# Mixer: the first head projected and activated ahead of the second half of the gates' chain, its queries, scores and an output gate ahead of the rows' transposes

## The chip, the cores and the metric

The kernel runs on one core of a Trainium2 chip. The metric is device time in microseconds (us); a kernel's time is the median of its runs. The core has five engines that run at the same time, each with its own queue: TensorE (PE, with its weight loads shown as PEld), VectorE (DVE), ScalarE (ACT), GpSimd (POOL) and SyncE (SP), which here issues most DMAs.

## The reference, cut to what matters

One layer of a diffusion backbone: a half-step SwiGLU, a mixer, another half-step SwiGLU, each between two RMS norms with modulation. There are 512 latent tokens and 256 context tokens of width 1024. The change lies in the mixer:

```python
p = y @ w_in                      # y: 768 tokens x 1024; columns: u (512), v (512), o (512), gates (16), pooling (512)
u = silu(short_conv(p_u))         # 3 taps along the tokens, 4 heads of 128
q, k = u @ w_q, u @ w_k           # per head
ig, fg = p_gates + biases         # 2 directions x 4 heads
# per direction and head, in chunks of 128 tokens:
#   b = cumsum(log_sigmoid(fg));  a running maximum m_t of decayed ig;  decays exp(.. - m_t)
#   num, den from (q k^T masked and decayed) v  and from a carried state;  h = num / max(|den|, exp(-m_t))
mix = concat(norm(h) * sigmoid(p_o), pool(p_pool))    # pool: box means of windows 2, 4, 8, 16 on the 8 x 64 grid
x = x + gate * norm(mix @ w_out)
```

## The kernel before, in words

**Products.** All large products are float32 split in a high and a low part, so each is three matmuls (`mm3p`). The normalised, modulated tokens lie as `yh`, `yl` (width across the partitions, 768 tokens along). A projection of 128 columns reads 8 weight blocks: `wcols` loads 1024 x 128 weights into a `raw` buffer (5 of them, by SP) and splits them (`split_w`) by a cast on ACT (L81) and a subtraction on DVE (L78) into two of 8 `wins` buffers, so that four sets of weights are there at a time.

**Stages.** The first SwiGLU ends, `values` projects v and the 16 gate columns (banks `pa`, `pz`, `pt` of PSUM: 4, 2 and 2). Then comes the mixer:

1. *The gates' chain* (L929 to L987), 64 rows x 768 tokens: three transposes twice, a log-sigmoid (ACT Exp L938 and Ln L939), two prefix sums on DVE (L950, L952), small copies that put the chunks' totals in place (L955 to L958), then what the change calls `gates`: three running-maximum scans (L959, L961, L963), small adds and copies into `mc` (L969 to L975), an Exp of `mc` (L976), the subtraction L978 and Exp L979 that make the rows `tr`, L980 to L983 for the rows' second half and for `br`, and `negmu` (L985 to L987). The order is by data: each step needs the one ahead of it.
2. *Rows to columns* (`rows_to_columns`): six transposes of `tr` in two `pt` banks, DVE copies out of them (L1011), four transposes of `br` in a third `pt` tile, copies (L1017), a selection matrix `sel` (L1022), `bd` (L1023), one small matmul and `cs_b` (L1028). All weights of keys, decays and states need these columns.
3. *Projections*: `u` is a head's input u (256 then 512 tokens, copied to `up` by ACT L1121, after DVE has zeroed its edges at L1117; then the convolution: ACT L1124 and two DVE instructions L1127; then ACT Silu L1129), `g` an output gate, `p` a pooling group. A group's sums run on POOL (L1053, L1100, L1101). `z` is the first half of the output product.
4. *Heads*: for each of the 4 heads queries `q` (a matmul, its ACT copy `qT` L1165, six transposes, two ACT copies L1171), scores `k` (four matmuls on `qT`, DVE products with the masks L1181), and for both directions weights `w`, states `s`, decays `d`, outputs `o`; then norm `n` and back `t`.

**Order.** `QUEUE` lists the projections, as generators that give PE one weight block of work at a time; `MIX` lists the heads' steps by letter, head and direction. `f2.4` draws some 2.4 us of work from the queue, `f` without a number draws until a pause (`.`), `R` is rows to columns, `P` a pooling group's second half. Matmuls and transposes of these steps keep the order of the program. On the other engines a planner sets the order ahead of time: among the instructions that its own model of the times takes as ready, the one that stands earlier in the program goes first. The order of each queue is then fixed, and an instruction that waits holds up those behind it. `tc.issue_after(x)` places what its block traces on `x`'s engine behind `x` in that engine's queue; it is an order, not a wait. Tiles of the mixer (`h` in the trace) come from `h4`, 16 buffers.

So before, PE gets pooling group 3, `u0` and `u1` ahead of `R`, then head 0's queries; the whole gates' chain stands ahead of all of these in the program.

Of the kernel before, what the change touches and what calls it, by code (L numbers as in the profile page):

```python
# [8 lines left out]
F32 = mybir.dt.float32  # L9
F32R = mybir.dt.float32r  # L10
# [6 lines left out]
P = 128  # L17
# [22 lines left out]
MIX = "f R q0 w00 f2.4 k0 s00 w01 d00 f0.4 f1.1 d01 s01 f3.35 o00 f3.45 q1 P3 o01 w10 k1 w11 f5.7 f2.25 s10 f0.1 f0.4 d10 s11 n0 f3.9 d11 f5.05 o10 f2.05 q2 w21 t0 P2 f2.8 w20 o11 n1 k2 f0.1 f0.1 s20 f2.95 d20 t1 f2.35 s21 d21 f2.15 o20 f1.6 P1 f1.25 o21 n2 f1.3 q3 w30 f2.15 t2 f1 w31 k3 d30 s30 f1.35 d31 s31 f2.65 o30 f0.1 f1.55 o31 n3 f0.1 f2 f0.1 P0 t3 f"  # L40


@with_exitstack
def tile_layer(ctx: ExitStack, tc: tile.TileContext, x, c, ctxt, c_ctx, w_mod, b_mod, norm_pre, norm_post,
# [855 lines left out]
    with ExitStack() as sx:  # L900
# [41 lines left out]
        def ch(tl, p0=0, p1=R):  # L942
# [15 lines left out]
        V.tensor_copy(ch(dr, 32, R)[:, 5:6, P - 1:P], ch(br, 32, R)[:, 0:1, 0:1])  # L958
        V.tensor_tensor_scan(out=mu[lo, 0:NT], data0=dr[lo, 0:NT], data1=ir[lo, 0:NT], initial=0.0,  # L959
                             op0=ALU.add, op1=ALU.max)  # L960
        V.tensor_tensor_scan(out=mu[hi, 0:NCTX][:, ::-1], data0=dr[hi, 0:NCTX][:, ::-1], data1=ir[hi, 0:NCTX][:, ::-1],  # L961
                             initial=0.0, op0=ALU.add, op1=ALU.max)
        V.tensor_tensor_scan(out=mu[hi, NCTX:NT][:, ::-1], data0=dr[hi, NCTX:NT][:, ::-1],  # L963
                             data1=ir[hi, NCTX:NT][:, ::-1], initial=mu[hi, 0:1], op0=ALU.add, op1=ALU.max)
# [4 lines left out]
        V.tensor_add(mcv[lo, 1:6], ch(dr, 0, 32)[:, 1:6, 0:1], ch(mu, 0, 32)[:, 0:5, P - 1:P])  # L969
        V.tensor_add(mcv[hi, 0:1], ch(dr, 32, R)[:, 0:1, P - 1:P], ch(mu, 32, R)[:, 1:2, 0:1])  # L970
        V.tensor_add(mcv[hi, 2:5], ch(dr, 32, R)[:, 2:5, P - 1:P], ch(mu, 32, R)[:, 3:6, 0:1])
        V.tensor_add(mcv[hi, 5:6], ch(dr, 32, R)[:, 5:6, P - 1:P], ch(mu, 32, R)[:, 0:1, 0:1])
        V.tensor_copy(mcv[lo, 12:18], ch(mu, 0, 32)[:, :, P - 1:P])
        V.tensor_copy(mcv[hi, 12:18], ch(mu, 32, R)[:, :, 0:1])
        V.tensor_sub(mc[:, 6:12], mc[:, 0:6], mc[:, 12:18])  # L975
        S.activation(out=mc[:, 6:12], in_=mc[:, 6:12], func=AF.Exp)  # L976

        V.tensor_sub(ch(tr), ch(ir), mcv[:, 12:18].broadcast_to([R, 6, P]))  # L978
        S.activation(out=t_, in_=t_, func=AF.Exp)  # L979
        V.tensor_copy(tr[R:2 * R, 0:NT], i_)  # L980
        LA = slice(NCTX, NT)
        V.tensor_add(br[0:R, LA], br[0:R, LA], mu[0:R, LA])
        S.activation(out=br[0:R, LA], in_=br[0:R, LA], func=AF.Exp, scale=-1.0)  # L983
        negmu = pool.tile([2 * R, NLAT], F32R, name="negmu")
        V.tensor_scalar_mul(mu[0:R, LA], mu[0:R, LA], -1.0)  # L985
        S.copy(negmu[0:R], mu[0:R, LA])
        V.tensor_sub(negmu[R:2 * R], mu[0:R, LA], negmu[0:R].bitcast(F32))  # L987

# [12 lines left out]
        bd = pool.tile([R, 8, 12], F32, name="bd")  # L1001
        cs_b = pool.tile([P, 8, 12], F32, name="cs_b")
        def rows_to_columns():

            for half in range(2):
                p = pt()
                for j in range(3):
                    tp(out=p[:, j * P:(j + 1) * P], in_=tr[:, (3 * half + j) * P:(3 * half + j + 1) * P],
                                identity=ident)
                for a in range(2):  # L1010
                    V.tensor_copy(tcol[:, 3 * half:3 * half + 3, a],  # L1011
                                  p[:, 0:384].rearrange("p (c a d r) -> p c a d r", c=3, a=2, d=2)[:, :, a, :, 0:4])
# [6 lines left out]
            selm = ident[0:R, 0:R].rearrange("p (d r) -> p d r", d=2)[:, :, 0:4]  # L1019
            for d in range(2):  # L1020
                for half in range(2):
                    V.tensor_copy(sel[half * R:(half + 1) * R, 4 * d:4 * d + 4], selm[:, d])  # L1022
# [27 lines left out]
        idhs, ups, uas, ogs = {}, {}, {}, {}  # L1050

# [3 lines left out]
        def pool_front(g):  # L1055

            win = WINDOWS[g]
            wts = wcols(PCOL + g * P)
            A = h4()[:, 0:GROWS * PW].rearrange("p (r c) -> p r c", c=PW)
# [406 lines left out]
```

## Time and profile before

| | |
|---|---|
| median of 3 runs | 1161.06 us (1160.05 to 1162.71) |
| the profiled execution | 1160.3 us |
| its span, first to last instruction | 1158.6 us |
| mean granted TensorE clock | 0.988 |
| busy: PE, PEld | 1107.9 us (96%), 1002.4 us (87%) |
| busy: DVE, ACT, POOL | 886.3 us (76%), 522.9 us (45%), 104.6 us (9%) |
| chain that ended last | PE 76%, DVE 9%, DMA 6%, ACT 3%, issue 2%, POOL 1% |

Busy is the time in which an engine ran at least one instruction. The granted clock is TensorE's as the throttle gave it, as a share of full speed. The chain is followed back from the last instruction, at each step to what released it. A row of a timeline gives a start, a duration, the engine, the source line, the operation and its operands, and in brackets how long the engine had been idle and what ended that.

### The profile page before, as it was taken

Reading aid. Unit: us, or ns where it says so; the run is one execution under the profiler, and the core shown is the slowest. Engines: PE = TensorE matmul, PEld = TensorE weight load, DVE = VectorE, ACT = ScalarE, POOL = GpSimd, SP = SyncE. Lnnn points to the kernel's source line nnn. Section 1 sums busy time; section 2 is a strip of 40 time slices with the busy share of each in tenths; the row PEclk is TensorE's granted clock in tenths of the full one; section 3 lists DMA queues with packets and bytes.
Section 4 is the critical chain, followed back from the end, with each engine's and each line's share of the span. In section 5 each row is a group of like instructions: output and inputs, shape, how many; then the busy total and the mean of one; then the engine's idle time right before and its main releaser. Section 6 shows DMA issues by size and latency. Waiting matters only on the chain.

```text
span 1158.6 us, 17190 instructions
## 1 busy us (share of the span) xinstructions
PE 1107.9 (96%) x6610; PEld 1002.4 (87%) x6610; DVE 886.3 (76%) x1309; ACT 522.9 (45%) x904; POOL 104.6 (9%) x139
## 2 busy tenths in 40 slices
PE   4999999999999999999899799999999999999996
PEld 2799999999998787888798687878899998999995
DVE  4698998898995685537628868856899998888865
ACT  4534333334333442326544755548554443444431
POOL 4000000000000000200205054211000000000001
PEclk9999999999999999999999899999999999999998
DMA  9943443542735896338513112135245544333321
GB/s 308 264 138 95 149 132 117 190 131 93 221 125 158 313 355 214 108 138 292 161 34 100 41 61 89 57 129 164 75 126 146 152 136 137 110 109 110 109 74 73
DMA packets 151807, 166.09 MB, mean 143 GB/s; under 512 B 7318, under 2 KB 125590, under 8 KB 151724
## 3 DMA queue, kind: packets, MB, share of 16 engines
q1 hardware_dynamic: 144708, 154.18, 42.0%
q10 hardware_dynamic: 7016, 10.80, 2.7%
q8 instruction: 52, 0.85, 0.3%
q14 instruction: 31, 0.25, 0.1%
HBM read 149.98 MB, written 14.98 MB: 142 GB/s over the span
## 4 chain that ended last, share of the span: by engine, by line
PE 76%; DVE 9%; DMA 6%; ACT 3%; issue 2%; POOL 1%; ACTq 0%; SPq 0%; DVEq 0%; POOLq 0%
PE pa L98 16%; PE pa L99 16%; PE pa L97 15%; PE pa L102 10%; PE pz L102 5%; PE pz L97 4%; DMA m<-in_w_mod_dram 3%; PE pz L98 3%; PE pz L99 3%; PE pt L102 3%; DVE wins L78 1%; DVE m L694 1%; PE pt L105 1%; ACT junk L148 1%; DMA raw<-in_w_mod_dram 1%
## 5 line engine op out<-in xcount | busy, mean ns | idle before, releaser
L97 PE MATMUL pa<-yh,wins 128*128 128x256 f32 (+1 forms) x768 | 236.4, 308 | 0.9 <-ACT pu L375 0.5
L98 PE MATMUL pa<-yh,wins 128*128 128x256 f32 (+1 forms) x768 | 235.9, 307 | 0.1
L99 PE MATMUL pa<-yl,wins 128*128 128x256 f32 (+1 forms) x768 | 235.6, 307 | 0.0
L78 DVE TENSOR_TENSOR wins<-raw,wins 128x1024 fp32r<-128x1024 f32 (+1 forms) x132 | 141.6, 1074 | 60.2 <-ACT wins L81 31.1
L81 ACT CAST wins<-raw 128x1024 fp32r<-128x1024 f32 (+1 forms) x134 | 123.0, 925 | 100.4 <-PE pa L99 35.0
L97 PEld LDWEIGHTS pa<-yh,wins 128*128 128x128 f32 x768 | 144.6, 188 | 4.1 <-ACT pu L375 1.1
L98 PEld LDWEIGHTS pa<-yh,wins 128*128 128x128 f32 x768 | 144.8, 188 | 0.9 <-DVE wins L78 0.3
L99 PEld LDWEIGHTS pa<-yl,wins 128*128 128x128 f32 x768 | 144.8, 189 | 0.3
L98 PE MATMUL pa<-th,wins 128*128 128x384 f32 (+1 forms) x388 | 121.9, 315 | 0.5 <-DVE wins L78 0.5
L99 PE MATMUL pa<-tl,wins 128*128 128x384 f32 (+1 forms) x388 | 122.2, 315 | 0.0
L97 PE MATMUL pa<-th,wins 128*128 128x384 f32 (+1 forms) x388 | 121.7, 315 | 0.0
L694 DVE SCALAR_TENSOR_TENSOR m<-m,sc,m 128x1024 f32<-128x1024 f32 x72 | 90.1, 1279 | 25.4 <-DMA m<-in_w_mod_dram 22.0
L81 ACT CAST wins<-sw 128x1024 fp32r<-128x1024 f32 x78 | 81.7, 1049 | 59.1 <-PE pa L99 33.9
L78 DVE TENSOR_TENSOR wins<-sw,wins 128x1024 fp32r<-128x1024 f32 x78 | 95.1, 1221 | 10.6 <-PE pa L98 8.6
L102 PE MATMUL pa<-yh,wins 128*128 128x512 f32 (+2 forms) x352 | 97.1, 362 | 0.0
L97 PEld LDWEIGHTS pa<-th,wins 128*128 128x128 f32 x388 | 72.9, 188 | 1.2 <-issue 0.8
L98 PEld LDWEIGHTS pa<-th,wins 128*128 128x128 f32 x388 | 73.2, 189 | 0.7 <-DVE wins L78 0.7
L99 PEld LDWEIGHTS pa<-tl,wins 128*128 128x128 f32 x388 | 73.1, 188 | 0.1
L102 PEld LDWEIGHTS pa<-yh,wins 128*128 128x128 f32 x352 | 62.1, 191 | 9.2 <-issue 2.2
L102 PE MATMUL pa<-yl,wins 128*128 128x512 f32 (+2 forms) x176 | 62.3, 354 | 0.0
L97 PE MATMUL pz<-wos,gh 128*128 128x512 f32 x144 | 56.6, 393 | 1.6 <-DVE z L429 1.1
L98 PE MATMUL pz<-wos,gl 128*128 128x512 f32 x144 | 56.3, 391 | 0.0
(409 smaller groups left out, 2198.0 us busy)
## 6 DMA issues: line engine op xcount, KB each, us to landing
raw<-in_ffn_w_in_dram SPq DMA_DIRECT2D x87, 512.0 KB
raw<-in_ffn_w_out_dram SPq DMA_DIRECT2D x56, 512.0 KB
m<-in_w_mod_dram SPq DMA_DIRECT2D x49, 512.0 KB
raw<-in_w_mod_dram SPq DMA_DIRECT2D x19, 512.0 KB
g<-q SPq DMA_DIRECT2D x22, 384.0 KB
q<-g ACTq DMA_DIRECT2D x44, 192.0 KB
raw<-in_w_in_dram SPq DMA_DIRECT2D x16, 512.0 KB
raw<-in_w_out_dram SPq DMA_DIRECT2D x16, 256.0 KB
```

The lines of the kernel that those rows point to most:

```text
L78: return eng.tensor_tensor(out=out_ap, in0=a, in1=b, op=ALU.subtract)
L81: return S.copy(hi, src)
L97: T.matmul(out_ap, lhsT=wh, rhs=xh, start=first, stop=False, **kw)
L98: T.matmul(out_ap, lhsT=wl, rhs=xh, start=False, stop=False, **kw)
L99: T.matmul(out_ap, lhsT=wh, rhs=xl, start=False, stop=last, **kw)
L102: return tc.keep_in_program_order(T.matmul(*args, **kw))
L105: return tc.keep_in_program_order(T.transpose(**kw))
L148: return S.activation(out=junk, in_=src, func=AF.Square, scale=D ** -0.5, accum_out=ssq)
L694: V.scalar_tensor_tensor(out=accs[st], in0=w, scalar=sc[:, st * KD + k:st * KD + k + 1], in1=accs[st], op0=ALU.mult, op1=ALU.add)
```

## The change

The second half of the gates' chain (from the first running-maximum scan on) becomes a function, `gates`, that is called at a new step `A`. The queue's first item is now `u0`, then a pause; `MIX` begins `f A f q0 k0 R w00`: draw `u0`, step `A`, draw group 3, `u1` and the output gate `g0`, then head 0's queries and scores, then rows to columns. Step `A` first makes the weights of group 3, of `u1` and of `g0` (`prefetch`), then traces `gates` behind head 0's Silu and behind the high cast of `g0`'s weights; both are on ACT, so both order ACT alone. In rows to columns the third and the fourth PSUM tile come from `pa` and `pz` instead of `pt`; the `sel` copies are traced ahead of it. `h4` gets 17 buffers. Seven numbers of `MIX` change: the first draw behind `w00` goes from 2.4 to 4.4, and six later ones become smaller by 0.6 to 1.8 each, 6.4 together.

```diff
-HB = 16
+HB = 17
-QUEUE = "p3 u0 u1 . u2 g0 p2 u3 g1 p1 g2 g3 p0 z"
-MIX = "f R q0 w00 f2.4 k0 s00 w01 d00 f0.4 f1.1 d01 s01 f3.35 o00 f3.45 q1 P3 o01 w10 k1 w11 f5.7 f2.25 s10 f0.1 f0.4 d10 s11 n0 f3.9 d11 f5.05 o10 f2.05 q2 w21 t0 P2 f2.8 w20 o11 n1 k2 f0.1 f0.1 s20 f2.95 d20 t1 ...
+QUEUE = "u0 . p3 u1 g0 . u2 p2 u3 g1 p1 g2 g3 p0 z"
+MIX = "f A f q0 k0 R w00 f4.4 s00 w01 d00 f0.4 f1.1 d01 s01 f3.35 o00 f2.45 q1 P3 o01 w10 k1 w11 f3.9 f2.25 s10 f0.1 f0.4 d10 s11 n0 f2.9 d11 f3.75 o10 f2.05 q2 w21 t0 P2 f2.1 w20 o11 n1 k2 f0.1 f0.1 s20 f2.35 d20 t1 ...
...
-        V.tensor_tensor_scan(out=mu[lo, 0:NT], ...
+        def gates():
+            V.tensor_tensor_scan(out=mu[lo, 0:NT], ...
...
+            V.tensor_sub(negmu[R:2 * R], mu[0:R, LA], negmu[0:R].bitcast(F32))
...
+        selm = ident[0:R, 0:R].rearrange("p (d r) -> p d r", d=2)[:, :, 0:4]
+        for d in range(2):
+            for half in range(2):
+                V.tensor_copy(sel[half * R:(half + 1) * R, 4 * d:4 * d + 4], selm[:, d])
         def rows_to_columns():
...
-            p = pt()
+            p = pa()
             for j in range(4):
                 tp(out=p[:, j * R:(j + 1) * R], in_=br[0:R, NCTX + j * P:NCTX + (j + 1) * P],
...
-            p = pt()
+            p = pz()
             mm(p[:, 0:96], lhsT=ones[0:R].broadcast_to([R, P]), rhs=bd..., start=True, stop=True)
...
+        casts = []
         def wcols(c0):
-            wh, wl = split_w(load_cols(w_in, c0))
+            wh, wl = split_w(load_cols(w_in, c0), keep=casts.append)
+        early_w = {}
+        def weights_of(c0):
+            return early_w.pop(c0, None) or wcols(c0)
+        def prefetch():
+            for c0 in (PCOL + 3 * P, P, 2 * M_W):
+                early_w[c0] = wcols(c0)
...
-            S.activation(out=u0, in_=u0, func=AF.Silu)
-            uas[h] = ua
+            silu = S.activation(out=u0, in_=u0, func=AF.Silu)
+            uas[h], silus[h] = ua, silu
...
+            elif what == "A":
+                prefetch()
+                with tc.issue_after(silus[0].ins), tc.issue_after(casts[-2].ins):
+                    gates()
```

`head_u`, `pool_front` and `out_gate` call `weights_of` in place of `wcols`.

## Rows read from the trace of the kernel before

**Rows 1.** The page's first part: busy time, share and instructions of each engine
```profile
PE 1107.9 (96%) x6610; PEld 1002.4 (87%) x6610; DVE 886.3 (76%) x1309; ACT 522.9 (45%) x904; POOL 104.6 (9%) x139
```

**Rows 2.** Windows: stretch, its length, busy of five engines, granted clock, DMA share, GB/s
```profile
638.00:640.00 2.00, 0.72 (x6) 0.64 (x6) 1.98 (x9) 1.62 (x3) 0.00 (x0) 0.99 0.00 0
640.00:650.00 10.00, 5.73 (x22) 4.22 (x21) 6.96 (x16) 8.30 (x13) 0.00 (x0) 0.50 0.30 71
650.00:760.00 110.00, 108.22 (x613) 91.29 (x613) 84.21 (x199) 63.85 (x147) 36.97 (x35) 1.00 0.20 64
```

**Rows 3.** Timeline of PE, 613 to 670: start, duration, engine, line, operation [idle before]
```profile
613.07 0.71 PE L102 MATMUL pa<-yh,wins 128*128 128x512 f32 x2
...
618.73 0.40 PE L102 MATMUL pa<-yh,wins 128*128 128x256 f32 x2
...
627.14 0.40 PE L102 MATMUL pa<-yh,wins 128*128 128x256 f32 x2
...
639.28 0.95 PE L105 MATMUL pt<-ident,h 128*128 128x128 f32 x6 [3.64 <-ACT h L979]
644.50 0.66 PE L105 MATMUL pt<-ident,h 64*128 64x64 f32 x4 [4.27 <-DVE tcol L1011]
...
645.57 2.07 PE L102 MATMUL pz<-h,wqk 128*128 128x512 f32 x2
...
648.58 0.78 PE L102 MATMUL pa<-yh,wins 128*128 128x256 f32 x2
...
652.22 1.05 PE L102 MATMUL pz<-h,h 128*128 128x128 f32 x8
653.11 1.28 PE L102 MATMUL pt<-vx,h 128*128 128x129 f32 x10
...
668.06 1.02 PE L102 MATMUL pz<-h,wqk 128*128 128x512 f32 x2
...
669.57 1.02 PE L102 MATMUL pz<-h,wp 128*128 128x512 f32 x2
```

**Rows 4.** Timeline of DVE, 619 to 696
```profile
619.08 0.95 DVE L940 SCALAR_TENSOR_TENSOR h<-h,h 64x768 f32<-64x768 f32 x1 [1.43 <-ACT h L939]
...
621.15 2.78 DVE L950 TENSOR_TENSOR_SCAN h<-h,h 32x768 f32<-32x768 f32 x1
...
629.66 2.31 DVE L959 TENSOR_TENSOR_SCAN h<-h,h 32x768 f32<-32x768 f32 x1
632.01 0.77 DVE L961 TENSOR_TENSOR_SCAN h<-h,h 32x256 f32<-32x256 f32 x1
...
635.26 1.16 DVE L970 TENSOR_TENSOR mc<-h,h 32x1 f32<-32x1 f32 x1
...
642.09 2.08 DVE L1127 SCALAR_TENSOR_TENSOR h<-h,pcol,h 128x770 f32<-128x770 f32 x2 [0.53 <-ACT h L1124]
...
694.34 1.78 DVE L1127 SCALAR_TENSOR_TENSOR h<-h,pcol,h 128x770 f32<-128x770 f32 x1
```

**Rows 5.** Timeline of POOL, 620 to 637
```profile
620.54 6.98 POOL L1053 TENSOR_TENSOR h<-h 128x624 f32<-128x624 f32 x3 [25.66 <-ACT h L1066]
...
634.34 2.07 POOL L1101 TENSOR_TENSOR h<-h,h 128x512 f32<-128x512 f32 x1
```

**Rows 6.** Timeline of ACT, 628 to 649
```profile
628.18 1.28 ACT L976 ACT_TABLE_LOAD   x1
...
638.38 0.84 ACT L979 ACTIVATE h<-h 64x768 f32<-64x768 f32 x1 [0.72 <-DVE h L978]
...
640.16 0.84 ACT L1121 COPY h<-pa 128x256 f32<-128x256 f32 x2
641.03 1.03 ACT L1124 ACTIVATE h<-h,pcol 128x770 f32<-128x770 f32 x1
...
647.68 0.59 ACT L1165 COPY h<-pz 128x512 f32<-128x512 f32 x1 [0.28 <-PE pz L102]
```

**Rows 7.** Timeline of SP's queue: issues of the projections' weights
```profile
559.11 19.86 SPq L114 DMA_DIRECT2D raw<-in_w_in_dram  x5
```

More of the change, by code (lines that the diff above doesn't have):

```diff
@@ L38 @@
 STEPS = "X0 E0 X1 X2 H00 Q0 H01 N0 N1 r00 G01 X3 r01 X4 N2 r02 r03 N3 b0 X5 Q1 N4 c0 N5 s01 y01 r10 E1 r11 s00 r12 r13 y00 b1 H10 G00 A10 H11 c1 Q2 A00 L11 G10 s11 y11 r20 A20 r21 r22 r23 A11 s10 y10 Q3 b2 c2 s20 y20 A21 r30 r31 r32 r33 A01 b3 s21 c3 s30 A02 y30 A22 y21 s31 A23 A03 y31 A12 A13"
-QUEUE = "p3 u0 u1 . u2 g0 p2 u3 g1 p1 g2 g3 p0 z"
-MIX = "f R q0 w00 f2.4 k0 s00 w01 d00 f0.4 f1.1 d01 s01 f3.35 o00 f3.45 q1 P3 o01 w10 k1 w11 f5.7 f2.25 s10 f0.1 f0.4 d10 s11 n0 f3.9 d11 f5.05 o10 f2.05 q2 w21 t0 P2 f2.8 w20 o11 n1 k2 f0.1 f0.1 s20 f2.95 d20 t1 f2.35 s21 d21 f2.15 o20 f1.6 P1 f1.25 o21 n2 f1.3 q3 w30 f2.15 t2 f1 w31 k3 d30 s30 f1.35 d31 s31 f2.65 o30 f0.1 f1.55 o31 n3 f0.1 f2 f0.1 P0 t3 f"
+QUEUE = "u0 . p3 u1 g0 . u2 p2 u3 g1 p1 g2 g3 p0 z"
+MIX = "f A f q0 k0 R w00 f4.4 s00 w01 d00 f0.4 f1.1 d01 s01 f3.35 o00 f2.45 q1 P3 o01 w10 k1 w11 f3.9 f2.25 s10 f0.1 f0.4 d10 s11 n0 f2.9 d11 f3.75 o10 f2.05 q2 w21 t0 P2 f2.1 w20 o11 n1 k2 f0.1 f0.1 s20 f2.35 d20 t1 f2.35 s21 d21 f2.15 o20 f1.6 P1 f1.25 o21 n2 f1.3 q3 w30 f2.15 t2 f1 w31 k3 d30 s30 f1.35 d31 s31 f2.65 o30 f0.1 f1.55 o31 n3 f0.1 f2 f0.1 P0 t3 f"
 @with_exitstack
@@ L958, in tile_layer @@
         V.tensor_copy(ch(dr, 32, R)[:, 5:6, P - 1:P], ch(br, 32, R)[:, 0:1, 0:1])
[L959 to L964, printed above, removed]
         mc = const.tile([R, 18], F32, name="mc")
@@ L968, in tile_layer @@
         mcv = mc.rearrange("p (a b) -> p a b", b=1)
[L969 to L980, printed above, removed]
-        LA = slice(NCTX, NT)
-        V.tensor_add(br[0:R, LA], br[0:R, LA], mu[0:R, LA])
-        S.activation(out=br[0:R, LA], in_=br[0:R, LA], func=AF.Exp, scale=-1.0)
@@ L984, in tile_layer @@
[L984 to L987, printed above, removed]
+        negmu = pool.tile([2 * R, NLAT], F32R, name="negmu")
+        LA = slice(NCTX, NT)
+        def gates():
+            V.tensor_tensor_scan(out=mu[lo, 0:NT], data0=dr[lo, 0:NT], data1=ir[lo, 0:NT], initial=0.0,
+                                 op0=ALU.add, op1=ALU.max)
+            V.tensor_tensor_scan(out=mu[hi, 0:NCTX][:, ::-1], data0=dr[hi, 0:NCTX][:, ::-1], data1=ir[hi, 0:NCTX][:, ::-1],
+                                 initial=0.0, op0=ALU.add, op1=ALU.max)
+            V.tensor_tensor_scan(out=mu[hi, NCTX:NT][:, ::-1], data0=dr[hi, NCTX:NT][:, ::-1],
+                                 data1=ir[hi, NCTX:NT][:, ::-1], initial=mu[hi, 0:1], op0=ALU.add, op1=ALU.max)
+            V.tensor_add(mcv[lo, 1:6], ch(dr, 0, 32)[:, 1:6, 0:1], ch(mu, 0, 32)[:, 0:5, P - 1:P])
+            V.tensor_add(mcv[hi, 0:1], ch(dr, 32, R)[:, 0:1, P - 1:P], ch(mu, 32, R)[:, 1:2, 0:1])
+            V.tensor_add(mcv[hi, 2:5], ch(dr, 32, R)[:, 2:5, P - 1:P], ch(mu, 32, R)[:, 3:6, 0:1])
+            V.tensor_add(mcv[hi, 5:6], ch(dr, 32, R)[:, 5:6, P - 1:P], ch(mu, 32, R)[:, 0:1, 0:1])
+            V.tensor_copy(mcv[lo, 12:18], ch(mu, 0, 32)[:, :, P - 1:P])
+            V.tensor_copy(mcv[hi, 12:18], ch(mu, 32, R)[:, :, 0:1])
+            V.tensor_sub(mc[:, 6:12], mc[:, 0:6], mc[:, 12:18])
+            S.activation(out=mc[:, 6:12], in_=mc[:, 6:12], func=AF.Exp)
+            V.tensor_sub(ch(tr), ch(ir), mcv[:, 12:18].broadcast_to([R, 6, P]))
+            S.activation(out=t_, in_=t_, func=AF.Exp)
+            V.tensor_copy(tr[R:2 * R, 0:NT], i_)
+            V.tensor_add(br[0:R, LA], br[0:R, LA], mu[0:R, LA])
+            S.activation(out=br[0:R, LA], in_=br[0:R, LA], func=AF.Exp, scale=-1.0)
+            V.tensor_scalar_mul(mu[0:R, LA], mu[0:R, LA], -1.0)
+            S.copy(negmu[0:R], mu[0:R, LA])
+            V.tensor_sub(negmu[R:2 * R], mu[0:R, LA], negmu[0:R].bitcast(F32))
@@ L1017, in rows_to_columns @@
             V.tensor_copy(gcol, p[:, 0:4 * R].rearrange("p (c d r) -> p c d r", c=4, d=2)[:, :, :, 0:4])
-            selm = ident[0:R, 0:R].rearrange("p (d r) -> p d r", d=2)[:, :, 0:4]
             for d in range(2):
-                for half in range(2):
-                    V.tensor_copy(sel[half * R:(half + 1) * R, 4 * d:4 * d + 4], selm[:, d])
                 V.tensor_tensor(out=bd[:, 4 * d:4 * d + 4],
@@ L1043, in project @@
                 yield n * 1.275e-3
+        casts = []
         def wcols(c0):
-            wh, wl = split_w(load_cols(w_in, c0))
+            wh, wl = split_w(load_cols(w_in, c0), keep=casts.append)
             return kc(wh), kc(wl)
+        early_w = {}
[4 more added lines that the diff above has]
+                early_w[c0] = wcols(c0)
         PW = GW + 16
-        idhs, ups, uas, ogs = {}, {}, {}, {}
+        idhs, uas, ogs, silus = {}, {}, {}, {}
         def padd(o, a, b):
@@ L1057, in pool_front @@
             win = WINDOWS[g]
-            wts = wcols(PCOL + g * P)
+            wts = weights_of(PCOL + g * P)
             A = h4()[:, 0:GROWS * PW].rearrange("p (r c) -> p r c", c=PW)
@@ L1112, in head_u @@
         def head_u(h):
-            wts = wcols(h * P)
+            wts = weights_of(h * P)
             up = h4()
@@ L1128, in head_u @@
                                        in1=u0, op0=ALU.mult, op1=ALU.add)
-            S.activation(out=u0, in_=u0, func=AF.Silu)
-            uas[h] = ua
+            silu = S.activation(out=u0, in_=u0, func=AF.Silu)
+            uas[h], silus[h] = ua, silu
         def out_gate(h):
-            wts = wcols(2 * M_W + h * P)
+            wts = weights_of(2 * M_W + h * P)
             q = pa()
```

## The prediction

> **What bounds the kernel now.** I read the page first: PE is busy 96% of the span [rows 1], so time is to be had only where PE idles or runs slowly. Cutting the mixer into windows finds one such place: in 640 to 650 PE is busy for 5.73 us of 10, and its granted clock is 0.50, the lower of two levels (1.2 of 2.4 GHz); in the 110 us behind it PE is busy for 108.22 at clock 1.00 [rows 2]. PE's timeline then shows three losses one behind the other [rows 3]:
>
> - Group 3, `u0` and `u1` are through at about 635.6. The transposes of the rows start at 639.28, after 3.64 us in which PE waits for ACT's Exp L979, the end of the gates' chain.
> - The next transposes start at 644.50, after 4.27 us. Both `pt` banks are taken, and the copies that empty them (L1011) stand on DVE behind the two convolution instructions of `u0` (642.09, 2.08 us [rows 4]).
> - PE had been idle before the clock fell, and what it does up to 650 runs at the lower level. 5.73 us of work there would take half, so this costs 5.73 / 2 = 2.87 us. Cross-check: the span from head 0's query matmul to the next step is 648.58 - 645.57 = 3.01, head 1's is 669.57 - 668.06 = 1.51 [rows 3].
>
> Together 3.64 + 4.27 + 2.87 = 10.78 us: what the change can win here.
>
> **What the change moves on PE.** Prices from the rows of PE: a group or a gate is 618.73 - 613.07 = 5.66 us, a `u` 627.14 - 618.73 = 8.41, queries 1.51, scores 653.11 - 652.22 = 0.89 [rows 3]. No matmul is added or dropped. From the same start, 613.07, the new order gives `u0` to 621.48, group 3 to 627.14, `u1` to 635.55, `g0` to 641.21, queries to 642.72, scores to 643.61, and only then `R`. That is 5.66 + 1.51 + 0.89 = 8.06 us more cover ahead of the rows. The third and fourth tile of `R` no longer use `pt`, so the second wait has no reason left; their own banks were last written by projections whose copies are short.
>
> **When the rows are ready now.** From the first running-maximum scan (629.66) to the first transpose (639.28) the chain takes 9.62 us [rows 3, 4]. Two things are put ahead of it on DVE: `u0`'s convolution, which now stands earlier in the program, 2.08 us; its edge memsets fit in the 1.43 us that DVE waits at 619 or cost hundredths. One thing goes: POOL's sums of group 3 started at 620.54 [rows 5] beside the two prefix sums, and start now after 627.14. The first sum took 2.78 us for 768 elements, where a scan of 256 took 0.77, so 2.31 for 768 [rows 4]: 0.47 each, some 0.9 for both. In exchange POOL's 15.9 us of sums (620.54 to 636.41 [rows 5]) now lie beside the whole second half up to about 643.6. What that does to DVE is seen later: a convolution instruction takes 1.78 us where its like took 1.04 [rows 4]. At 0.74 us for each of the three long instructions of the tail (L978, L980, L982) it is 0 to 2.2. Rows ready: 639.28 + 2.08 - 0.9 + (0 to 2.2), 640.5 to 642.7; I take 641.4, nearer the low end, since the scans ran beside POOL before as well. PE wants them at 643.61, so the first wait is covered with 2.2 us to spare, and 0.9 at the worse end.
>
> **What the order on ACT adds.** `gates`' four ACT instructions stand behind head 0's Silu. `u0` is projected at 621.48; copies (0.84), L1124 (1.03) [rows 6], 2.08 on DVE between or behind the prefix sums, a Silu of under 1 us: done between 627 and 635, depending on whether DVE's first half runs to its end first. One table load is added, since Silu now comes between Ln and the gates' Exps: 1.28 us [rows 6]. Up to about 637 ACT has nothing else that is urgent, so I cost both at 0; if the Silu came after 637, each us would go straight to the rows. The cast of `g0`'s weights is no burden: the five loads were issued from 559.11 on, in 19.86 us [rows 7], with the first four sets in place at the start of the projections; `prefetch` changes which set comes first, not how many, and the loads behind them keep their places on SP. POOL's queue gets nothing new, the sums only start later.
>
> **What is late next.** Scores wait for ACT's copy `qT`. Alone it is 0.59 us [rows 6] beside the queries' transposes, a wait of 0.1 or so. But on ACT `u1` stands earlier in the program: two copies and L1124, 0.84 + 1.03 = 1.87 us [rows 6], and they are likely to become ready just then, when the chain lets DVE do `u1`'s edges. If the planner also puts `u1`'s Silu ahead of `qT`, with its table load (1.28) and the two DVE instructions that it waits for (2.08), the wait is 0.1 + 1.87 + 1.28 + 2.08 = 5.3, and the copies of `un`, which free `pt` for `R`, are as late. Bounds 0.1 to 5.3. I take 1.5: in the trace `qT` stood behind a L1124 and still came 0.28 us after its matmul [rows 6], with no Silu between.
>
> **Heads.** `g0` and the first scores, 6.55 us, leave the stretch behind `R`; six draws shrink. DVE's 84.21 us in 110 [rows 2] become 84 in about 103.5, 81% instead of 77%. PE's idle there was 1.78 us. Behind each step some us of other work remain, so I take 0.3, with bounds from -1.8 (the idle vanishes) to 4. The 17th buffer, the earlier `sel` and the renamed banks cost nothing: no instruction is added.
>
> **Sum.** 10.78 - 1.5 - 0.3 = 9.0 us. Against the profiled execution's own time (1160.3, that is 1.7 around its span of 1158.6) this gives 1151.3. The median of the runs is 0.8 above that execution, so the forecast for the median is 1161.06 - 9.0 = 1152.0. Work behind the mixer is bound by PE, so nothing there swallows it.
>
> **Rivals.**
>
> *Handover late* (16%): `qT` and `un` stand behind `u1`'s Silu, or the rows come 2 us later than the range above. PE waits about 4 us at the scores or at `R`; the like wait of 3.64 us stood before the fall to clock 0.50, so the 2.87 us of half clock come back too. Gain 10.78 - 4 - 2.87 = 3.9: 1157.1. For it: the planner's order on ACT is not known. Against it: a Silu is ready only after two DVE instructions, the copies at once.
>
> *Given back in the heads* (9%): less filling makes the steps of heads 1 and 2 wait for DVE, 4 to 5 us in all, gain 5 to 6: 1155.5. For it: 81% of DVE on average. Against it: PE idled 1.78 us in 110 with the old filling.
>
> *Blocked by POOL, slower* (6%): L970, on 32 x 1 elements, took 1.16 us and ended at 636.42, as POOL's L1101 ended at 636.41 [rows 4, 5]. So a DVE instruction can stand until a POOL instruction ends. If each of some ten instructions from L959 to L982 lost 0.9 us in that way, the rows would come at 641.4 + 9 = 650.4, PE would idle 6.8 us and then run a stretch as before at half clock (2.9); with 3 us given back in the heads that is 10.78 - 12.7 = -1.9, 1163. It decides from rows at about 649.5 on. The Trainium skill (SBUF — State Buffer, "Who interferes with whom") speaks for it: a Vector instruction with two SBUF inputs and a GpSimd instruction that reads SBUF exclude each other for a whole instruction. By that rule the second half, now wholly beside POOL, would stand longer than I count. The trace agrees for L970, and not for L950, whose 2.78 us lie beside POOL from end to end and are only 0.47 above the clean rate.
>
> *It doesn't do what it says* (4%): the planner leaves `u0`'s convolution behind the scans on DVE. Head 0's Silu then ends near 645, as the old order has it (642.09 + 2.08 and a Silu), the Exps and the rows come at 647 to 648, PE idles some 4 to 5 us and falls to half clock for the queries, scores and `R`: 10.78 - 5 - 4.5 = 1.3 gained, 1159.8.
>
> **How the numbers follow.** The forecast's case holds 65%, its own range 1149.6 (the idle in the heads goes too) to 1154.5. The range of 8 in 10 reaches to both middle cases: 1149.6 to 1157.4. A measurement of this kernel tells 0.2%, 2.3 us, from no change. Faster by more: the first case and nearly all of the next two, 0.88. Within: 0.06, from *It doesn't do what it says* and the edge of its neighbours. Slower: 0.06.
>
> **What would show it.** Right: PE without a gap from 613 to the end of `R`, clock 1.00 throughout, the first transposes of `tr` about 643 to 645, the second four right behind them, `u2` at 645 to 647. The order: DVE does L1127 twice ahead of L959 or between L959 and L963; ACT shows Silu ahead of L976. The wait in question stands on the scores (`pz<-h,h`), ended by ACT L1165. Wrong: a clock of 0.50 anywhere in 640 to 660, L979 later than 643, or more than 4 us of PE idle in the 105 us behind `R`.

## The result: slower by 0.6%, and the profile after

The changed kernel took 1168.5 us (median of 6 runs, 1166.3 to 1170.8), the one before 1162.2 on the same chip: ratio 1.0059, 95% interval [1.0042, 1.0075]; that is 6.3 us more between the medians, 6.9 by the ratio. Forecast were 1152.0 and a range of 1149.6 to 1157.4. In the profiled executions the span grew from 1158.6 to 1164.5, although the chain of gates began 0.79 us earlier in the one after (the transposes at its start: 612.20 for 612.99), so the mixer and what follows cost 6.7 us.

The line numbers below are those of the changed kernel, up to 20 higher than before: the Exp of the rows L979 is L984, the convolution step L1127 is L1146, head 0's copy `qT` L1165 is L1184, the sums L1053 are L1072. The page's first part answers to [rows 1]; PE's share fell from 96 to 95%:

```profile
PE 1111.5 (95%) x6610; PEld 1004.3 (86%) x6610; DVE 882.9 (76%) x1309; ACT 522.2 (45%) x905; POOL 100.8 (9%) x139
```

The windows of after, to be read against [rows 2] (stretch, length, busy time of PE, PEld, DVE, ACT and POOL, granted clock, DMA share, GB/s):

```profile
640.00:650.00 10.00, 6.27 (x33) 4.92 (x32) 6.27 (x13) 4.01 (x7) 8.31 (x10) 0.83 0.34 92
650.00:760.00 110.00, 101.75 (x568) 84.35 (x567) 79.71 (x185) 57.94 (x135) 34.70 (x32) 0.98 0.18 56
...
645.00:650.00 5.00, 4.28 (x22) 3.78 (x23) 2.47 (x10) 2.38 (x5) 3.52 (x4) 0.66 0.00 0
686.00:692.00 6.00, 4.99 (x20) 4.47 (x21) 5.57 (x17) 3.73 (x7) 5.30 (x4) 0.72 0.21 61
760.00:775.00 15.00, 13.64 (x56) 10.16 (x56) 8.40 (x19) 7.29 (x17) 1.22 (x2) 0.89 0.55 176
```

Two things are to be seen. The hole at 640 to 650 is smaller, not gone. And the 110 us behind it, which PE used to fill to 108.22, now hold 101.75: the change did win something at its place, and gave more than that back in the heads. At 760 to 775 the kernel before was busy for 14.97 at clock 1.00:

```profile
760.00:775.00 15.00, 14.97 (x65) 11.33 (x64) 9.11 (x12) 7.42 (x14) 0.77 (x1) 1.00 0.53 176
```

PE's timeline of after (answers to [rows 3]; columns as there). The first rows are the new order, head 0's queries, scores and only then the rows' transposes; the last two are the steps of heads 1 and 2 that now wait:

```profile
640.32 1.02 PE L102 MATMUL pz<-h,wqk 128*128 128x512 f32 x2
...
645.72 1.65 PE L102 MATMUL pz<-h,h 128*128 128x128 f32 x8 [3.73 <-ACT h L1184]
647.17 1.49 PE L105 MATMUL pt<-ident,h 128*128 128x128 f32 x6
648.59 0.69 PE L105 MATMUL pa<-ident,h 64*128 64x64 f32 x4
...
687.01 2.34 PE L102 MATMUL pt<-vx,h 128*128 128x129 f32 x10 [3.33 <-DVE st L1220]
...
714.77 1.35 PE L102 MATMUL pt<-vx,h 128*128 128x129 f32 x10 [2.13 <-DVE h L1266]
```

The rows' transposes (647.17) and the next (648.59) have no wait any more: both old waits are gone. In their place the scores wait 3.73 us for `qT`. ACT's timeline (answers to [rows 6]) says why:

```profile
629.33 0.85 ACT L1148 ACTIVATE h<-h 128x770 f32<-128x770 f32 x1 [2.63 <-DVE h L1146]
...
633.13 0.85 ACT L984 ACTIVATE h<-h 64x768 f32<-64x768 f32 x1 [0.66 <-DVE h L983]
...
634.92 0.57 ACT L1085 COPY h<-pa 128x512 f32<-128x512 f32 x1
...
643.87 0.85 ACT L1148 ACTIVATE h<-h 128x770 f32<-128x770 f32 x1 [3.36 <-DVE h L1146]
644.62 0.58 ACT L1156 ACTIVATE og<-pa 128x512 f32<-128x512 f32 x1
645.09 0.58 ACT L1184 COPY h<-pz 128x512 f32<-128x512 f32 x1
```

The Exp that the rows need ends at 633.98, 13 us before PE's transposes of the rows start (647.17). But the second head's Silu (643.87) stands ahead of the output gate's activation (L1156) and of `qT`, and ACT idles 3.36 us for its convolution. On DVE (answers to [rows 4]) the scans are short now, 1.75 us for what took 2.31 to 2.78, and the two convolution steps that ACT waits for are long, 3.86 us for what took 2.08:

```profile
619.27 1.75 DVE L950 TENSOR_TENSOR_SCAN h<-h,h 32x768 f32<-32x768 f32 x1
...
639.98 3.86 DVE L1146 SCALAR_TENSOR_TENSOR h<-h,pcol,h 128x770 f32<-128x770 f32 x2
...
683.91 2.29 DVE L1278 TENSOR_TENSOR h<-h,sm 128x512 f32<-128x512 f32 x1 [3.25 <-POOL sm L143]
```

POOL's timeline (answers to [rows 5]) is the other half of it: group 3's sums, 620.54 before, start at 635.58, behind the copy L1085 that ACT got to only after the gates' four instructions, and so lie beside the second convolution and no longer beside the scans. Group 2's sums start at 671.59, and its later parts stand around the two small instructions of head 0's norm:

```profile
635.58 5.50 POOL L1072 TENSOR_TENSOR h<-h 128x624 f32<-128x624 f32 x3 [53.56 <-ACT h L1085]
...
671.59 2.29 POOL L1072 TENSOR_TENSOR h<-h 128x560 f32<-128x560 f32 x2 [22.88 <-ACT h L1085]
...
680.05 0.66 POOL L1276 TENSOR_SCALAR sm<-sm 128x4 f32<-128x4 f32 x1 [4.43 <-ACT h L1274]
680.79 2.10 POOL L1072 TENSOR_TENSOR h<-h 128x896 f32<-128x896 f32 x1
682.84 1.03 POOL L143 TENSOR_TENSOR sm<-sm,mhalf 128x4 f32<-128x4 f32 x1
```

Read the last three with DVE's 683.91 and PE's 687.01: the norm's power (682.84) stands behind a sum of 2.10 us, DVE idles 3.25 us for it, its product of the norm takes 2.29 us where the same instruction took 0.69 elsewhere, and the state update queued behind it (L1220) is what PE's 3.33 us wait for.

### The profile page after: what moved, and what is told of

It is laid out like the page before. It is cut to its first block, busy times and chain, and to the rows that moved or that the text cites. A ratio compares the mean times of both kernels' runs of the same rounds, so it can differ in the third digit from the quotient of the medians.

```text
span 1164.5 us, 17185 instructions
## 1 busy us (share of the span) xinstructions
PE 1111.5 (95%) x6610; PEld 1004.3 (86%) x6610; DVE 882.9 (76%) x1309; ACT 522.2 (45%) x905; POOL 100.8 (9%) x139
## 4 chain that ended last, share of the span: by engine, by line
PE 72%; DVE 8%; issue 7%; DMA 5%; POOL 3%; ACT 3%; ACTq 0%; SPq 0%; DVEq 0%; POOLq 0%
PE pa L98 16%; PE pa L99 16%; PE pa L97 16%; PE pa L102 7%; PE pz L102 4%; PE pz L97 4%; PE pz L98 4%; PE pz L99 4%; DMA m<-in_w_mod_dram 3%; PE pt L102 2%; POOL h L1072 1%; DVE wins L78 1%; PE pt L105 1%; DVE m L694 1%; DMA raw<-in_w_mod_dram 1%
```

## The experiments

All were timed against the kernel before on the same chip, whose median was 1160.6 to 1161.4 there; the changed kernel stands at ratio 1.0059. Below, "the theory" is this one: the change loses in two places, the order on ACT at the handover to `qT`, and GpSimd's sums, which now come at other times. Rivals: too little filling behind the steps; or the three losses of before were no losses of order at all.

**Head 1's convolution behind head 0's queries.** In `head_u` the part from the convolution to the Silu becomes a function, run for head 1 in a step of its own:

```
-MIX = "f A f q0 k0 R w00 f4.4 ...
+MIX = "f A f q0 k0 R w00 C f4.4 ...
+            if h == 1:
+                late_u.append(convolve)
+            else:
+                convolve()
...
+            elif what == "C":
+                with tc.issue_after(heads[0].un_copy.ins):
+                    late_u.pop()()
```

> The changed kernel with head 1's convolution and Silu issued later: traced behind head 0's first weights, its ACT instructions behind head 0's last un copy. Theory 'two queues': qT no longer stands on ACT behind that Silu, the 3.73 us before the scores and the stretch at clock 0.66 behind it go, about 5 us: some 1163.5, no PE idle at the scores. The wait of 3.33 us ahead of the second states of head 1 stays. Rival 'too little filling': the time won at the scores is lost again at the next steps of the heads, since the draws were cut by 6.4 us; 1167 to 1169.

Measured: 1161.8 us, ratio 1.0008 [0.9996, 1.0019], so 0.51% better than the change alone. PE's waits at the scores and at head 1's states:

```profile
644.05 1.16 PE L102 MATMUL pz<-h,h 128*128 128x128 f32 x8 [0.36 <-ACT h L1192]
...
684.11 2.49 PE L102 MATMUL pt<-vx,h 128*128 128x129 f32 x10 [3.32 <-DVE st L1228]
```

The first fell from 3.73 to 0.36, the second stayed: the second doesn't come from the first.

**The sums of groups 2 and 1 behind the norms.** In `pool_front` everything from the first sum on becomes a function, run for two of the groups behind the norm of heads 0 and 1:

```
-... d10 s11 n0 f2.9 ... o11 n1 k2 ...
+... d10 s11 n0 S2 f2.9 ... o11 n1 S1 k2 ...
+            elif what == "S":
+                with tc.issue_after(heads[2 - int(arg)].pow.ins):
+                    late_sums.pop(int(arg))()
```

> The changed kernel with the POOL sums of pooling groups 2 and 1 issued behind the two small POOL operations of the norms of heads 0 and 1. Theory 'two queues': DVE's norm product no longer waits 3.25 us for POOL, the waits of 3.33 us (second states of head 1) and 0.81 us (back of head 1) go, with the slow clock behind them 5 to 6 us: about 1163. The 3.73 us at the scores stay. Rival 'too little filling': the states wait for DVE all the same, 1167 to 1169.

Measured: 1163.5 us, ratio 1.0016 [1.0005, 1.0027], 0.43% better than the change. The wait at the states is gone, the scores' 3.73 us stay, and a new one has come, behind four VectorE instructions that are slow beside the sums. PE, then DVE of this run:

```profile
700.19 0.49 PE L102 MATMUL pt<-vx,h 128*128 128x129 f32 x2 [3.00 <-DVE h L1245]
```

```profile
692.35 2.46 DVE L1154 SCALAR_TENSOR_TENSOR h<-h,pcol,h 128x770 f32<-128x770 f32 x1
...
694.99 1.79 DVE L1154 SCALAR_TENSOR_TENSOR h<-h,pcol,h 128x770 f32<-128x770 f32 x1
696.71 1.75 DVE L1246 TENSOR_TENSOR h<-h,h 128x512 f32<-128x512 f32 x1
698.38 1.75 DVE L1245 TENSOR_TENSOR h<-h,h 128x512 f32<-128x512 f32 x1
```

The same instructions take 1.02, 1.02, 0.69 and 0.69 us when POOL is idle. So the order on POOL was the cause of the wait at 687, and moving the sums moves the damage to what lies beside them.

**Both edits.**

> Both edits on the changed kernel. Theory 'two queues': the gains add up, 10 to 11 us: 1157 to 1158, faster than the kernel before by 4 to 5. Rival 'too little filling': 1164 or more, with new waits of several us between 670 and 730 that end on DVE.

Measured: 1159.5 us, ratio 0.9984 [0.9969, 0.9999]. Alone the edits gave back 0.51% and 0.43%, together 0.75%, most of the sum, and they take the change to just below the kernel before, not to the 1157 to 1158 us that I had expected; the 3.00 us wait at the outputs of head 1 stays.

**The later draws as before** (the rival of too little filling): six `f` steps of `MIX` get their old lengths back, in the changed kernel and in the one with both edits.

```
-... o00 f2.45 ... w11 f3.9 ... n0 f2.9 ... d11 f3.75 ... P2 f2.1 ... s20 f2.35 ...
+... o00 f3.45 ... w11 f5.7 ... n0 f3.9 ... d11 f5.05 ... P2 f2.8 ... s20 f2.95 ...
```

> The changed kernel with the six later draws of MIX as before (3.45, 5.7, 3.9, 5.05, 2.8, 2.95), the first at 4.4. Theory 'two queues': the wait at the scores (3.73 us) and the one behind POOL (3.33 us) stay, since neither comes from the draws; smaller ones in heads 1 and 2 shrink; 1165 to 1168. Rival 'too little filling': the waits in the heads go, 1160 to 1162.

> Both edits of e3 (Silu of head 1 behind, sums of groups 2 and 1 behind the norms) and the six later draws as before. In e3 PE still waits 3.0 us at the outputs of head 1 and 1.6 us at the back of head 1, both on DVE. If these come from too little work between the steps, they shrink: 1155 to 1157, some 3 us below e3. If they come from DVE being stretched by POOL beside it, they stay and the end has less work left: 1159 to 1161.

Measured: 1171.2 us, ratio 1.0083 [1.0068, 1.0098], and with both edits 1165.2, 1.0036 [1.0023, 1.0049]. Both are slower, against the rival, and slower than either side had expected. Two views of the first of the two show how. POOL: group 2's sums are now issued whole ahead of head 0's norm, which waits until all are through; the window is that of 760 to 775, where PE now works only 8.60 us of 15:

```profile
676.87 8.04 POOL L1072 TENSOR_TENSOR h<-h 128x512 f32<-128x512 f32 x4
...
688.70 1.04 POOL L143 TENSOR_TENSOR sm<-sm,mhalf 128x4 f32<-128x4 f32 x1
```

```profile
760.00:775.00 15.00, 8.60 (x49) 7.00 (x48) 8.45 (x26) 5.76 (x17) 1.39 (x2) 0.88 0.31 106
```

With both edits, where group 2's sums stand behind the norm, PE works 11.16 us in the same window, against 13.62 with the short draws. The filling is a fixed stock. What `g0` took ahead of the rows is missing at the end if the draws in between stay as long as they were. In this order, shrinking the draws was right.

**The banks alone.** The kernel before, with `R`'s third and fourth tile in the banks that the change uses:

```
-            p = pt()
+            p = pa()
             for j in range(4):
                 tp(out=p[:, j * R:(j + 1) * R], ...
...
-            p = pt()
+            p = pz()
             mm(p[:, 0:96], ...
```

> The kernel before with one part of the change alone: the third and fourth PSUM tile of rows to columns come from pa and pz. As the prediction counted (the 4.27 us wait is for the pt bank and goes with it): 4.3 us and half of the slow clock less, about 1156. Theory now: PE would then wait for head 0's Silu (it ended at 645.05, the query matmul started at 645.57), so the wait only moves from the transposes to the queries: less than 1 us, 1161 to 1162.

Measured: 1160.5 us, ratio 0.9996 [0.9982, 1.0009]. The second wait of before [rows 3] went away as I had said, and stood again one step later:

```profile
642.57 2.07 PE L102 MATMUL pz<-h,wqk 128*128 128x512 f32 x2 [3.19 <-ACT h L1129]
```

4.27 us had two ends, the bank and head 0's Silu; the renamed banks take off about one of the four.

**Without the sums.** To price them, the box sums on GpSimd are left out, in the changed kernel and in the one before; the buffers that they fill become free with them, so this price isn't that of the slowing alone:

```
-            src = A
...
-                tot = o[:, 6:7, :].broadcast_to([P, GROWS, GW])
+            tot = A[:, :, 8:8 + GW]
             G.tensor_tensor(out=inv, in0=tot, in1=inv, op=ALU.mult)
```

> The changed kernel without the adds of the box sums on POOL (all four groups; the scaling and the subtraction stay). Theory 'two queues', with DVE stretched by POOL: head 1's convolution beside it goes from 3.86 to 2.1 us, so the wait at the scores falls from 3.73 to 1 to 2 us, the wait behind POOL goes: 1157 to 1159. Rival 'too little filling': 1165 or more.

> The kernel before without the same adds on POOL: what POOL costs there. The two prefix sums and the maximum scans no longer lie beside POOL, the gates' chain is some 4 us shorter, so the first wait (3.64 us) goes nearly all, the wait for head 0's Silu follows: 4 to 6 us less than before, 1156 to 1158, about the same as the changed kernel without the sums. If POOL cost nothing before: 1161 to 1162.

Measured: the changed kernel 1154.1 us, ratio 0.9948 [0.9933, 0.9962]; the one before 1150.6, 0.9914 [0.9900, 0.9928]. So the sums, all on an engine that is busy 9% of the span, cost about 10 us in the kernel before (0.86% of 1161) and 13 in the changed one (1.0059 - 0.9948 = 1.11%). Both times are below what I had expected (1157 to 1159 and 1156 to 1158). And without the sums the change still costs 3.5 us. Of the kernel before without sums, PE at the rows, the 10 us there and the 110 us behind (its scans took 1.74 and 1.75 us):

```profile
635.87 0.81 PE L105 MATMUL pt<-ident,h 128*128 128x128 f32 x6
640.20 0.43 PE L105 MATMUL pt<-ident,h 64*128 64x64 f32 x4 [3.52 <-DVE tcol L1011]
```

```profile
640.00:650.00 10.00, 9.80 (x61) 8.43 (x62) 6.64 (x16) 6.89 (x11) 0.63 (x1) 0.83 0.21 56
650.00:760.00 110.00, 109.77 (x605) 91.61 (x603) 81.45 (x198) 65.29 (x150) 16.43 (x16) 1.00 0.22 72
```

The first wait, 3.64 us, is gone with no change of PE's order: it was the chain stretched by the sums. The second is still 3.52 us, and the clock behind it 0.83 over the 10 us. Of the changed kernel without sums, PE at the scores, the second convolution on DVE, and the same 110 us:

```profile
642.23 1.26 PE L102 MATMUL pz<-h,h 128*128 128x128 f32 x8 [2.11 <-ACT h L1187]
```

```profile
638.27 2.07 DVE L1149 SCALAR_TENSOR_TENSOR h<-h,pcol,h 128x770 f32<-128x770 f32 x2
```

```profile
650.00:760.00 110.00, 106.95 (x595) 88.74 (x595) 81.56 (x196) 64.69 (x149) 16.00 (x16) 1.00 0.23 74
```

The convolution takes 2.07 us again, and of the 3.73 us at the scores 2.11 are left: the order on ACT alone. The handover is no cheaper for it, since the lower clock lasts longer: 642.2 to 649.8 holds 7.58 us of work at 0.56, where with the sums 645.7 to 649.7 holds 3.98 at 0.57. Wait and clock together come to 2.11 + 3.3 us, against 3.73 + 1.7. The heads idle 3.05 us of 110, at clock 1.00, where the kernel before without sums idles 0.23. By elimination I put that part of the heads' loss down to the filling used up early; no run gives the filling back.

**Without the sums, and head 1's convolution late.** The edits of the first and of the last experiment in one.

> The changed kernel without the box sums on GpSimd (the scaling and the subtraction stay) and with head 1's convolution behind head 0's queries. Without the sums the changed kernel took 1154.1 us and the one before 1150.6. Theory (what is then left against the change is head 1's convolution ahead of the copy of head 0's queries, a wait of 2.1 us, and the clock of 0.66 behind it): the wait falls under 0.5 us and the time is 1150.5 to 1152, about that of the kernel before without sums: the change's three wins are in it, but they are no longer there to be won where the chain runs clean. Rival (the change itself wins what I forecast as soon as both costs are gone): 1146 to 1149.

Measured: 1152.3 us, ratio 0.9927 [0.9915, 0.9939], a little over the range that the theory gave; the wait at the scores is 0.36. The rival, that the change wins its 9 us as soon as both defects are gone, is refuted: even then it doesn't beat the kernel before without sums (0.9914 [0.9900, 0.9928]). What it wins at the rows it gives back, most of it in the heads, where PE idles 3.28 us:

```profile
650.00:760.00 110.00, 106.72 (x589) 87.93 (x588) 82.84 (x198) 66.72 (x151) 16.00 (x16) 1.00 0.21 67
```

**Group 3's sums later, in the kernel before.** The same edit as above for group 3, its sums emitted behind `R` and ordered behind the chain's last instruction:

```
-MIX = "f R q0 ...
+MIX = "f R S q0 ...
+            elif what == "S":
+                with tc.issue_after(last_gate.ins):
+                    late_sums.pop(3)()
```

> The kernel before, with one edit: GpSimd's sums of group 3 are not issued as its projection lands but behind the last instruction of the gates' chain (about 641 us). Theory (the sums stretch VectorE instructions beside them, and the first wait, 3.64 us for the last exponential, is mostly the chain's scans running beside them): the scans take 1.75 us each and the transposes find their rows, so the first wait goes; the second, 4.27 us, stays at 3 to 4, as it ends with head 0's convolution, which now has the sums beside it; 1158 to 1159.5 us. Rival (the first wait is the order of the work on PE, as my forecast had it): the wait stays over 3 us and the time at 1161.

Measured: 1158.9 us, ratio 0.9986 [0.9977, 0.9996]. The test failed as a test: the order asked for binds instructions of one engine only, the chain's last instruction is on DVE, and POOL started its sums as before:

```profile
621.83 5.76 POOL L1054 TENSOR_TENSOR h<-h 128x624 f32<-128x624 f32 x3 [27.85 <-ACT h L1067]
```

```profile
638.15 0.88 PE L105 MATMUL pt<-ident,h 128*128 128x128 f32 x6 [3.41 <-ACT h L979]
```

The wait for the rows stayed; that the time lies in the range that the theory gave says nothing. In the next version data hold the sums: a small GpSimd instruction ahead of the sums reads head 0's activated columns.

```
+                touch = small(4)
+                read = G.tensor_scalar(out=touch, in0=uas[0][:, 0:4], scalar1=1.0 / P, scalar2=EPS, ...)
+                with tc.issue_after(read.ins):
+                    late_sums.pop(3)()
```

> The kernel before, with GpSimd's sums of group 3 held by data: a small GpSimd instruction ahead of them reads head 0's activated columns, ready at about 647 us. Theory (the first wait, 3.64 us, was the gates' chain stretched beside the sums): scans of 1.75 us, transposes without a wait, the second wait still 3 to 4.5; the sums, now at 647 to 663, stretch head 1's convolution, for which nothing waits before 669; 1157 to 1159 us against 1161. Rival (PE's order makes the first wait, as my forecast had it): it stays over 3 us and the time at 1160 to 1161; or the sums, late, hold up PE at group 3's way back, about 671: 1161 or more.

Measured: 1156.05 us (1155.2 to 1156.4), ratio 0.9959 [0.9946, 0.9972], with all sums in it: faster than both kernels. POOL, DVE and PE of this run:

```profile
639.20 5.23 POOL L1054 TENSOR_TENSOR h<-h 128x624 f32<-128x624 f32 x3
...
644.89 3.80 POOL L1054 TENSOR_TENSOR h<-h 128x512 f32<-128x512 f32 x4
```

```profile
621.47 1.74 DVE L950 TENSOR_TENSOR_SCAN h<-h,h 32x768 f32<-32x768 f32 x1
...
641.43 3.81 DVE L1135 SCALAR_TENSOR_TENSOR h<-h,pcol,h 128x770 f32<-128x770 f32 x2
645.16 2.02 DVE L1196 TENSOR_TENSOR h<-un,tcol 128x768 f32<-128x768 f32 x1
```

```profile
638.28 0.43 PE L105 MATMUL pt<-ident,h 64*128 64x64 f32 x4 [1.68 <-DVE tcol L1011]
...
647.33 2.12 PE L102 MATMUL pt<-vx,h 128*128 128x129 f32 x10 [2.91 <-DVE h L1125]
```

The scans are clean, the first wait is gone, the second is 1.68 for 4.27, and a new one of 2.91 us has come where the sums now lie: the row names DVE's memset L1125, the instruction that ends just there; the long ones on DVE ahead of it are the convolution and the weighting L1196, 2.02 us for 0.95. Head 0's Silu, and with it the sums, came 8 us sooner than I had put them (639 for 647), because the chain ahead of it had become shorter.

**Head 3's convolution late too**, in the changed kernel with both edits: from beside group 2's sums to behind that group's way back.

```
-            if h == 1:
+            if h in (1, 3):
...
-... P2 f2.1 w20 ...
+... P2 f2.1 w20 D ...
```

> The changed kernel with head 1's convolution behind head 0's queries and the sums of groups 2 and 1 behind the norms, and besides head 3's convolution moved from beside group 2's sums to behind group 2's way back. Theory (what is left of the loss there is VectorE work stretched beside the sums: the convolution's two steps took 2.46 and 1.79 us where 1.02 is usual, and PE waited 3.0 us behind them): that wait falls under 1.0 us and the time from 1159.5 to 1156.5 to 1158. Rival (the wait moves to the next VectorE instruction beside the sums and the time stays): 1159 to 1160.

Measured: 1158.3 us, ratio 0.9984 [0.9972, 0.9995], the same ratio as without it (0.9984 [0.9969, 0.9999]). The 3.00 us wait is gone, as the theory has it; the gain isn't to be seen, as the rival has it: PE now waits for head 2's masked scores, which stand on DVE behind the product of head 1's norm, 1.56 us beside group 1's sums for 0.69 without:

```profile
711.07 1.09 PE L105 MATMUL pz<-ident,h 128*128 128x128 f32 x4 [2.52 <-DVE h L1216]
```

So group 1's sums were held by data until those are written:

> The version with head 1's and head 3's convolutions late and the sums of groups 2 and 1 behind the norms, and besides the sums of group 1 held by data until head 2's masked scores are written (about 712 us). Theory (PE's wait of 2.52 us at 711 was those masked scores and the instructions ahead of them on VectorE beside the sums of group 1): it falls under 1.0 us, and the time from 1158.3 to 1156.5 to 1157.5. Rival (VectorE's queue is full there without the sums): the wait stays over 2 us and the time at 1158 to 1159.

Measured: 1157.25 us, ratio 0.9971 [0.9961, 0.9980]. The time lies in the range that the theory gave. The wait at 711 is gone; two others are there:

```profile
709.29 1.35 PE L102 MATMUL pt<-vx,h 128*128 128x129 f32 x10 [2.04 <-DVE h L1282]
...
723.10 0.49 PE L102 MATMUL pt<-vx,h 128*128 128x129 f32 x2 [2.11 <-DVE h L1253]
```

At the first of them GpSimd had been idle until 710.02, so it isn't the sums: VectorE's own queue is late there, as the rival has it. Whether this beats the version before it (0.9984) isn't settled, the intervals overlap. It does beat both kernels; its median is behind that of the old order with group 3's sums held, but these intervals overlap too.

**The mixer alone.** In the profiled executions the mixer begins at different times: the last of the transposes that open the gates' chain (L930) start between 610.33 and 615.75. So I also read the time from there to the start of the transposes `pt<-ident,raw` behind the mixer, which wait some 0.7 us for DVE's L187 (781.40 before, 787.88 after), in one execution of each:

| version | mixer, us |
|---|---|
| before; changed | 168.4; 175.7 |
| changed, head 1's convolution late; sums behind the norms; both | 171.0; 173.4; 167.4 |
| changed with the old draws; with both edits and the old draws | 179.0; 171.9 |
| before, banks alone | 167.7 |
| no sums: before; changed; changed, convolution late | 160.5; 164.5; 160.7 |
| before, group 3's sums ordered; held by data | 168.4; 164.0 |
| changed, both edits and head 3's convolution late; group 1's sums held besides | 166.6; 165.8 |

Read so, the sums cost 7.9 us in the kernel before and 11.2 in the changed one, the two edits give back 4.7 and 2.3 us alone and 8.3 together, and the version that only ordered the sums is as long as the kernel before, so that its 0.14% is no gain. Not tested: the changed kernel with group 3's sums held off head 1's convolution, and other draws for the changed order without sums.

## Why the prediction was wrong

By its own terms, from the windows and waits above (a stretch at a granted clock c is counted as costing busy time x (1 - c), as the 2.87 us of before were):

| term | forecast, us | found, us |
|---|---|---|
| the three losses at 635 to 650 | +10.78 | +10.78 |
| what is late next, at the scores | -1.5 | -5.2 (3.73 and 4.28 x 0.34 = 1.46) |
| heads, 650 to 760 | -0.3 | -7.9 (108.22 - 101.75 = 6.47 and 4.99 x 0.28 = 1.40) |
| the mixer's end, 760 to 775 | 0 | -2.8 (1.33 and 13.64 x 0.11 = 1.50) |
| sum | +9.0 | -5.1, measured -6.7 |

A window is fixed in time while the work in it shifts, so some 1.6 us I can't place. No run isolates the loss at the mixer's end; without the sums PE idles 0.72 us there, at clock 1.00, in both orders.

**The step that failed** is *Heads*: "Behind each step some us of other work remain, so I take 0.3, with bounds from -1.8 (the idle vanishes) to 4". It was 7.9, and its cause stands two paragraphs earlier in the prediction, in a cost put at nothing: "POOL's queue gets nothing new, the sums only start later". I looked at group 3 alone. With `g0` gone from the filling, group 2 is projected sooner and its sums start at 671.59, 9.4 us earlier than the 680.97 us of the kernel before, so that head 0's norm is queued among them. The second experiment takes that wait away. Without the sums the change costs the heads 3.05 - 0.23 = 2.8 us, a size that my bound of 4 did hold (by elimination, filling used ahead of its time); about 5 of the 7.9 come with the sums.

**What is late next** was a mis-sized term with the right mechanism and the right bound: the planner did put the second Silu ahead of `qT`, the case that I had priced at 5.3 and given up for 1.5, because in the trace of before `qT` came soon behind an L1124 "with no Silu between"; against the rival I held that "a Silu is ready only after two DVE instructions, the copies at once". On the chip that was so: the queries' matmuls ended at about 641.3, the Silu could start only at 643.87. But the queue's order had been fixed ahead of time, with the Silu first, as in the program; what times the planner's model gave the two isn't shown. As *Handover late* I had given it 16%; its price, 4 and the half clock, was near what came (3.73 and 1.46). The first experiment shows it: 0.36 us of wait with the Silu behind.

**The rows** were 7.4 us earlier than my 641.4 (0.8 of it from the earlier start), outside 640.5 to 642.7, and that in spite of head 0's convolution between the scans. I took 2.31 us as the clean duration of a 768-element scan, three times the 0.77 of 256 elements; that one lay beside POOL too, as did L959 with its 2.31, and the clean durations are 0.68 and 1.75. And group 3's sums did not start "after 627.14", where its matmuls ended, but at 635.58: ACT's copy stood behind head 0's Silu and the gates' four instructions, an engine's queue that I had costed for the rows and not for this copy.

That also turns round what I made of the rule of the Trainium skill (SBUF — State Buffer, "Who interferes with whom"). By row L950 I had found it 0.47 us over the clean rate and held the rule refuted there. With the clean 1.75 us it is 1.03 over, the two convolution steps in the run with group 3's sums held by data and the weighting behind them 1.73 / 2 = 0.87 and 1.07 over, against 0.95 for one of the GpSimd sums there (3.80 / 4). So the trace agrees with the rule, that an instruction with two SBUF inputs and one of GpSimd's that reads SBUF shut each other out: the excess is about one GpSimd instruction.

**The winnable time.** I read the three losses as losses of order. The first was 3.64 us because the chain was stretched, and was to be had without reordering PE; the second ended with head 0's Silu as much as with the bank. The new order did remove all three. But without sums, with the second Silu late, the two orders come out alike (0.9927 and 0.9914; the mixer 160.7 and 160.5), although the old one still waits 3.52 us and then runs at the lower clock there: most of what the new order wins at the rows comes back as idle time in the heads, 3.28 against 0.23. As drawn up here, the order itself won nothing.

**The rivals.** *Blocked by POOL, slower* had 6%: the right engine at the wrong place. It put the block on the chain, which ran clean; it was on the second convolution, on the norms and on the products in the heads. Its time, 1163, was nearer than mine. *Given back in the heads* (9%) had the right place and 4 to 5 us for the 7.9.

**What held.** PE's order to the queries: forecast 642.72 - 1.51 = 641.21 from a start at 613.07, measured 640.32 from one at 612.29. No wait at the transposes. Head 0's convolution between the scans, its Silu at 629.33 (forecast 627 to 635), and the added table load at no cost.

## What to carry to other kernels

Before an engine's instruction durations are used as clean ones, look at what ran beside them on VectorE's and GpSimd's side; here the sums of an engine that is busy 9% of the span cost 8 to 10 us, much of it through the instructions that they slow: holding back group 3's, with none dropped, gave 4.4 of it. When work is drawn forward out of a filling, follow everything that the filling carried into every queue (here a group's sums into GpSimd's, ahead of small instructions on the critical path), and ask which later stretch loses it. Where two consumers of an engine become ready close together, allow for the order of the program becoming the order of the queue, and test the cheap remedy first: holding the one bulk producer back by data gave 0.4%, the reordering lost 0.6% and came to a gain of 0.3% only with four more edits.

## What I had not expected of the hardware

VectorE instructions beside GpSimd's sums, this kernel's runs, us alone and beside them: scan of 32x768 1.75 and up to 2.78; convolution step of 128x770 1.02 and 2.46; product of 128x512 0.69 and 1.75. An instruction with an input in PSUM is not slowed: the 32 state updates of 128x129 took 0.33 to 0.35 us each in the kernel before, those beside the sums too. One with a single SBUF input is: the output gate's scaling of 128x512, 0.42 us alone, took 1.81 beside them in the run with head 3's convolution late. It goes both ways: a GpSimd sum of 128x512 took 8.04 / 4 = 2.01 us beside two-input VectorE instructions in the run with the old draws; in the last version of the kernel before such a sum took 0.95, and there VectorE's weighting beside it did the waiting (2.02 us for 0.95).
